# Differential-attention scores as 64-row products on both halves of the array, and the gates' columns turned one pair later

## The chip, the cores and the metric

The kernel runs on one core of a Trainium2 chip. The core has a matrix engine (TensorE; PE in the profile, its weight loads PEld), VectorE (DVE), ScalarE (ACT), GpSimd (POOL) and SyncE (SP), which here issues nearly all DMAs. The metric is the device time of one execution in microseconds, as the median of several runs.

## The reference

One layer on a sequence of 1024 rows and 1024 features: a normalisation, a projection to all segments, two branches (an mLSTM in both directions with 4 heads of 256, and a differential attention with 8 heads), a gated mix of the two, an output projection and a final normalisation. The change is in the attention branch. A head has two query and two key parts (j = 0, 1) of 64 features each, turned by a rotary embedding, and values of 128 features:

```
scores = jnp.einsum('bqhjd,bkhjd->bhjqk', qb, k) * scale
p = jax.nn.softmax(scores, axis=-1)
p_diff = p[:, :, 0] - lam * p[:, :, 1]
return jnp.einsum('bhqk,bkhd->bqhd', p_diff, v)
```

All is in 32-bit floating point.

## The kernel before, in words

**Precision.** A 32-bit product is made of products of a reduced 32-bit type. An operand x is split into a high part H (a rounded copy, by ScalarE) and a low part L = x - H (by GpSimd or VectorE), and a product is taken as HH + HL + LH, three products on TensorE that accumulate in one PSUM bank.

**Stages.** The normalised input stays in SBUF as hH and hL, transposed. First come the mLSTM's projections (`pair_units`, L286), sixteen pairs of weight columns by a scheme with fewer products; pairs alternate between convolution pairs (aq, ak) and output-gate pairs. Small steps are put between these units by a table of (pair, place): the mLSTM's gates (`ml_gates`: rows, chain, weights, columns) and the rotary tables (`ang`). `columns` turns four gate rows blocks and a decay row into columns with 64-row transposes (L131) into banks T and copies them out on VectorE (L810, L817). Then comes the attention (461 to about 1110 us), then the mLSTM, then the two mixes and the output.

**Attention.** `da_proj` makes q and k of a head in two halves of 512 columns (L424 products), turns them (L847 to L865) and leaves them in tile `hl`: partitions 0 to 63 are q of j = 0 and 1, 64 to 127 are k, with 32 rows for each half of the rotation; four slices hold H and L of the two halves. Through a DRAM tile `stk` (four writes, L868) these rows are stacked anew: `qq` gets q's 64 rows of a j twice, on partitions 0 to 63 and again on 64 to 127 (two loads, L870), and `kst` gets H of k on the upper 64 partitions and L of k on the lower ones (L871). So one product of 128 rows with H of q gives HH + HL, and a second with L of q gives LH + LL: four products of 512 columns for the 1024 keys of one j (L918).

For a query tile t of 128 rows, `scores(t, j)` takes a two-bank PSUM tile S (two such tiles exist), makes these four products, takes the negated row maximum (VectorE, L920), the exponential with its row sum (ScalarE, L922), and with j = 1 the combination of both (L927 to L929). `transposes(t, g)` turns half of the combined tile through the single bank T (L131), ScalarE rounds it to pH (L942) and VectorE makes pL (L943). `pv` multiplies with the values for two tiles at a time (L954), `squares`, `finish`, `spread` and `scale` normalise the head's result; `spread` is a DMA that broadcasts a row to all partitions as `rb`, on SP's queue, and `scale` (L997) waits for it.

**Order.** TensorE's order is fixed by a planner, `Weaver`. Each `Unit` has a nominal cost (MM = 0.214 for a product of 512 columns, TP = 0.109 for a transpose), may hold a bank (`tag`, `hold`) and may have to wait a nominal time after another unit (`after`, from the table `LAG`). `da_cycle` lists the units of one tile; `weave` merges that list with the fill (projections of the next head, gates) by which unit is ready first, then by the share of its list that is done. A unit's own costs and holds say nothing to the chip: they set the order alone. The other engines' orders are made by the compiler's scheduler.

Of the kernel before, what the change touches and what calls it, by code (L numbers as in the profile page):

```python
# [28 lines left out]
def two_pi_parts():  # L29
# [9 lines left out]
MM = 0.214  # L39
TP = 0.109  # L40

LAG = dict(Th=2.2, Sh=3.2, PVh=3.7, Mh=8.1, Fh=5.0, qk=14.0, T=6.8, PV=3.7, M=4.5, F=0.4, TTh=1.9, TT=3.2, POh=1.6,
           PO=1.7, Wh=0.3, W=2.0, STh=2.1, ST=4.9, th=1.8, t=4.1, aq=9.0, outh=6.6, out=14.0, G=18.9)


# [64 lines left out]
class Block:  # L110
# [726 lines left out]
    def da_proj(self, h, st):  # L837
        A, v, a, p, q = self.A, self.v, self.a, self.p, self.q
        w1 = self.w1
        fb = lambda x: x.bitcast(F32)  # L840
        kA, kB = ("rope", h, 0), ("rope", h, 1)

        def first(half, pa):
            c = slice(half * 512, (half + 1) * 512)
            m = [w1.tile([128, 512], F32, name=f"m{i}", tag=f"m{i}", bufs=1) for i in range(2)]
            st["m"] = m
            v.tensor_tensor(out=m[0], in0=pa, in1=self.cosT[:, c], op=ALU.mult)  # L847
            v.tensor_tensor(out=m[1], in0=pa, in1=self.sinT[:, c], op=ALU.mult)

        def second(half, pb):  # L850
            c = slice(half * 512, (half + 1) * 512)
            if half == 0:
                st["k"] = w1.tile([128, 2, S], F32R, name="kst", tag="kst", bufs=2)
            qq = w1.tile([128, 4, 512], F32R, name="qq", tag="qq", bufs=3)
            st["q", half] = (qq[:, 0::2], qq[:, 1::2])
            m = st["m"]

            hl = w1.tile([128, 4, 512], F32R, name="hl", tag="hl", bufs=1)
            v.tensor_tensor(out=fb(hl[:, 2]), in0=pb, in1=self.sinT[:, c], op=ALU.mult)
            v.tensor_tensor(out=fb(hl[:, 3]), in0=pb, in1=self.cosT[:, c], op=ALU.mult)  # L860
# [42 lines left out]
    def da_parts(self, h, st):  # L903
        v, a, p, q, w1 = self.v, self.a, self.p, self.q, self.w1

        def scores(t, j):
            if t == 0 and j == 0:
# [3 lines left out]
            qH, qL = st["q", t // 4]  # L911
            c = slice((t % 4) * 128, (t % 4) * 128 + 128)
            Z = st["Z"]
            ps = self.bank("S", (128, S))
            for x, first in ((qH, True), (qL, False)):
                for kh in range(2):
                    o = slice(kh * 512, (kh + 1) * 512)
                    self.t.matmul(ps[:, o], lhsT=x[:, j, c], rhs=st["k"][:, j, o], start=first, stop=not first)  # L918
            nm = w1.tile([128, 1], F32, name="nm", tag="nm", bufs=3)
            v.tensor_reduce(out=nm, in_=ps, axis=AX.X, op=ALU.max, negate=True)  # L920
            e = w1.tile([128, S], F32, name=f"e{j}", tag=f"e{j}", bufs=2 if j == 0 else 1)
            a.activation(out=e, in_=ps, func=AF.Exp, bias=nm[:, 0:1], accum_out=Z[:, j, t:t + 1])  # L922
            st["e", j] = e
            if j == 1:
                e0 = st["e", 0]
                r = w1.tile([128, 1], F32, name="r", tag="r", bufs=1)
                v.reciprocal(out=r, in_=Z[:, 1, t:t + 1])  # L927
                v.tensor_scalar(out=r, in0=r, scalar1=Z[:, 0, t:t + 1], scalar2=self.nlam[:, 0:1], op0=ALU.mult, op1=ALU.mult)
                v.scalar_tensor_tensor(out=e0, in0=e, scalar=r[:, 0:1], in1=e0, op0=ALU.mult, op1=ALU.add)  # L929
                st["p", t] = e0  # L930

        def transposes(t, g):
            pt = st["p", t]
# [61 lines left out]
        def scale(half):  # L995
# [7 lines left out]
        return dict(  # L1003
            S=lambda t, j: Unit(4 * MM, lambda: scores(t, j), tag="S", hold=LAG["Sh"], name=("S", h, t, j), after=((("qk", h), LAG["qk"]),)),
            T=lambda t, g: Unit(4 * TP, lambda: transposes(t, g), tag="T", hold=LAG["Th"], name=("T", h, t, g),
                                after=((("S", h, t, 1), LAG["T"]),)),
            PV=lambda t2, g: Unit(12 * TP, lambda: pv(t2, g), tag="PV" if g == 0 else None, hold=LAG["PVh"], name=("PV", h, t2, g),
                                  after=((("T", h, 2 * t2 + 1, g), LAG["PV"]),)),
            M=lambda t2: Unit(2 * TP, lambda: squares(t2), tag="PV", hold=LAG["Mh"], name=("M", h, t2),
                              after=((("PV", h, t2, 1), LAG["M"]), (("z", h if t2 == 3 else -1), 0.0))),  # L1010
# [3 lines left out]
    @staticmethod  # L1014
    def da_cycle(cur, prev, t):

        before = cur if t > 0 else prev
        un = []
        if cur:
            un.append(cur["S"](t, 0))  # L1020
        own = cur if t >= 4 else prev
        if own and t % 2 == 0:
            un.append(own["M"]((t // 2 - 2) % 4))
        if prev and t in (4, 6):
            un.append(prev["G"](t // 2 - 2))
# [12 lines left out]
        return un  # L1038
# [403 lines left out]
    def build(self):  # L1442
# [21 lines left out]
        with pool(name="const", bufs=1) as self.const, \  # L1464
# [51 lines left out]
            w = Weaver()  # L1516
# [137 lines left out]
```

## Time and profile before

| | us |
|---|---|
| median of 3 runs | 1732.61 (1730.03 to 1735.3) |
| the profiled execution | 1731.73 |
| its span in the profile | 1730.0 |
| mean granted TensorE clock | 0.990 |
| TensorE products busy | 1661.3 (96%) |
| weight loads busy | 1417.5 (82%) |
| VectorE, ScalarE, GpSimd busy | 998.4, 783.6, 603.4 |

A row of instructions in order of time reads: start, shown length, engine, line, operation, out<-in, rows*columns of the weights, and the shape that streams. A product's end is modelled, so consecutive products overlap in the shown lengths; the distance between starts is what a product takes. In a table by stretch the columns are busy time and count of PE, PEld, DVE, ACT and POOL, the granted clock, the DMA share and GB/s.

### The profile page before, as it was taken

To read this page: it belongs to the slowest core of one execution; us is meant where nothing else is said; L and a number is where in the kernel's file an instruction comes from. 1 tells how busy PE (TensorE), PEld (TensorE's weight loads), DVE (VectorE), ACT (ScalarE), POOL (GpSimd) and SP (SyncE) were. 2 spreads that over 40 slices of the span, in tenths; PEclk is the share of its full clock that TensorE was granted. 3 is DMA by queue.
4 is the path that set the end of the run, shared out by engine and by line. 5 is a ranking of instruction groups with operands and counts; after the bars stand their busy time and mean duration, and the time that the engine had idled before them with its cause. 6 is when DMAs were issued, how large, how long until landed. Compare 5 with 4: busy or idle time off the path is not lost. (4 is left out here: it accounts for less than half of the span.)

```text
span 1730.0 us, 24692 instructions
## 1 busy us (share of the span) xinstructions
PE 1661.3 (96%) x9119; PEld 1417.5 (82%) x9119; DVE 998.4 (58%) x1855; ACT 783.6 (45%) x1562; POOL 603.4 (35%) x608
## 2 busy tenths in 40 slices
PE   7999998999999999999999999989999989999998
PEld 5777886887887987898889878879999877888887
DVE  5678677674267666666676665425666743226533
ACT  7455554553245444445545445424655743122221
POOL 4767665665232224322441331222312311222000
PEclk9999999999999999999999999999999999999999
DMA  5343433435443514441635152146455327444222
GB/s 181 93 136 112 143 114 122 122 122 153 126 98 84 144 56 117 117 121 38 170 74 135 44 158 68 61 150 199 140 157 157 89 87 247 143 144 136 86 85 86
DMA packets 190092, 208.15 MB, mean 120 GB/s; under 512 B 12249, under 2 KB 135538, under 8 KB 189970
## 3 DMA queue, kind: packets, MB, share of 16 engines
q1 hardware_dynamic: 189058, 204.98, 40.2%
q8 instruction: 72, 1.18, 0.3%
q10 hardware_dynamic: 912, 1.59, 0.2%
q14 instruction: 50, 0.41, 0.1%
HBM read 143.47 MB, written 63.05 MB: 119 GB/s over the span
## 5 line engine op out<-in xcount | busy, mean ns | idle before, releaser
L424 PE MATMUL pj<-hH,wH 128*128 128x512 f32 x640 | 257.7, 403 | 6.3 <-ACT wH L188 3.1
L424 PE MATMUL pj<-hH,wL 128*128 128x512 f32 x640 | 252.6, 395 | 2.6 <-POOL wL L202 1.7
L424 PE MATMUL pj<-hL,wH 128*128 128x512 f32 x640 | 252.4, 394 | 0.2 <-DVE hL L575 0.2
L922 ACT ACTIVATE e<-S,nm 128x1024 f32<-128x1024 f32 x128 | 143.1, 1118 | 170.2 <-DVE nm L920 169.8
L204 POOL TENSOR_TENSOR wL<-raw,wH 128x1024 fp32r<-128x1024 f32 x41 | 101.0, 2463 | 295.1 <-ACT wH L199 290.2
L920 DVE TENSOR_REDUCE nm<-S 128x1 f32<-128x1024 f32 x128 | 155.7, 1217 | 21.3 <-PE S L918 21.2
L943 DVE TENSOR_TENSOR pL<-T,pH 128x512 fp32r<-128x512 f32 x128 | 87.9, 687 | 138.4 <-ACT pH L942 138.4
L918 PE MATMUL S<-kst,qq 128*128 128x512 f32 x512 | 151.4, 418 | 1.3 <-DMA kst<-stk 1.3
L446 PE MATMUL pj<-wH,hH 128*128 128x256 f32 x512 | 147.7, 288 | 0.3
L424 PEld LDWEIGHTS pj<-hH,wH 128*128 128x128 f32 x640 | 121.6, 190 | 31.1 <-ACT wH L188 3.5
L424 PEld LDWEIGHTS pj<-hH,wL 128*128 128x128 f32 x640 | 121.2, 189 | 30.8 <-POOL wL L202 3.1
L446 PE MATMUL pj<-wL,hH 128*128 128x256 f32 x512 | 145.0, 283 | 1.4 <-POOL wL L202 1.4
L446 PE MATMUL pj<-wH,hL 128*128 128x256 f32 x512 | 144.6, 282 | 0.0
L424 PEld LDWEIGHTS pj<-hL,wH 128*128 128x128 f32 x640 | 121.3, 189 | 23.4 <-DVE hL L575 0.6
L424 PE MATMUL pj<-sl_yb,wH 128*128 128x512 f32 x384 | 120.7, 394 | 4.4 <-ACT sl_yb L1327 2.3
L199 ACT CAST wH<-raw 128x1024 fp32r<-128x1024 f32 x56 | 58.8, 1050 | 120.8 <-PE pj L424 111.1
L918 PEld LDWEIGHTS S<-kst,qq 128*128 128x128 f32 x512 | 90.6, 193 | 15.3 <-DMA kst<-stk 1.8
L446 PEld LDWEIGHTS pj<-wL,hH 128*128 128x128 f32 x512 | 97.7, 191 | 2.3 <-POOL wL L202 2.3
L446 PEld LDWEIGHTS pj<-wH,hH 128*128 128x128 f32 x512 | 97.9, 191 | 1.6 <-ACT wH L199 0.7
L446 PEld LDWEIGHTS pj<-wH,hL 128*128 128x128 f32 x512 | 97.8, 191 | 0.9
L929 DVE SCALAR_TENSOR_TENSOR e<-e,r,e 128x1024 f32<-128x1024 f32 x64 | 94.7, 1480 | 1.3
L189 POOL TENSOR_TENSOR wL<-raw,wH 128x512 fp32r<-128x512 f32 x32 | 40.7, 1290 | 154.5 <-ACT wH L188 149.1
(357 smaller groups left out, 4127.9 us busy)
## 6 DMA issues: line engine op xcount, KB each, us to landing
raw<-in_w_in_dram SPq DMA_DIRECT2D x88, 512.0 KB
stk<-hl SPq DMA_DIRECT2D x64, 256.0 KB
qq<-stk SPq DMA_DIRECT2D x32, 512.0 KB
kst<-stk SPq DMA_DIRECT2D x16, 512.0 KB
x<-in_x_dram SPq DMA_DIRECT2D x8, 512.0 KB
cak<-y SPq DMA_DIRECT2D x16, 256.0 KB
cakH<-cin SPq DMA_DIRECT2D x16, 256.0 KB
cakL<-tz SPq DMA_DIRECT2D x16, 256.0 KB
```

The lines of the kernel that those rows point to most:

```text
L189: self.p.tensor_tensor(out=vw(wL), in0=src, in1=vw(wHf), op=ALU.subtract)
L199: self.a.copy(wH, raw)
L204: self.p.tensor_tensor(out=wL, in0=raw, in1=wHf, op=ALU.subtract)
L424: self.t.matmul(ps, lhsT=l[:, k, :], rhs=r, start=(n == 0), stop=(n == 23))
L446: self.t.matmul(ps[:, i, :], lhsT=l, rhs=r[:, k, :], start=(kh == 0 and k == 0 and m == 0), stop=(kh == 1 and k == 3 and m == 2))
L918: self.t.matmul(ps[:, o], lhsT=x[:, j, c], rhs=st["k"][:, j, o], start=first, stop=not first)
L920: v.tensor_reduce(out=nm, in_=ps, axis=AX.X, op=ALU.max, negate=True)
L922: a.activation(out=e, in_=ps, func=AF.Exp, bias=nm[:, 0:1], accum_out=Z[:, j, t:t + 1])
L929: v.scalar_tensor_tensor(out=e0, in0=e, scalar=r[:, 0:1], in1=e0, op0=ALU.mult, op1=ALU.add)
L943: v.tensor_tensor(out=pL[:, :, s], in0=ps, in1=pH[:, :, s].bitcast(F32), op=ALU.subtract)
```

## The change

`hl` goes to DRAM by (H or L, half of the rotation), one write for each of its four slices over all 128 partitions. `qq` now has H and L of q with j = 0 on the upper 64 partitions and j = 1 on the lower ones, and `kst` has the same for k: one load each. `scores(t)` takes both PSUM tiles and makes for each half of the keys and each of HH, HL and LH one product of 64 rows for j = 0 and one for j = 1, in turns; the product LL is no longer made. Maxima, exponentials and the combination follow as before, both maxima now after one unit. In the planner a tile has one score unit of 6 MM in place of two of 4 MM, S is one holding of 5.0 instead of two of 3.2, and the transposes wait 6.8 after that unit. In `da_cycle` the second score unit between the two transpose units is gone. Apart from this, the five steps of `columns` go from pair 9, places 8 to 12, to pair 10, places 5, 7, 9, 11 and 13, between steps of `ang` at 4 to 12.

```
-            qq = w1.tile([128, 4, 512], F32R, name="qq", tag="qq", bufs=3)
-            st["q", half] = (qq[:, 0::2], qq[:, 1::2])
+            qq = st["q", half] = w1.tile([128, 2, 512], F32R, name="qq", tag="qq", bufs=3)
...
-            dr = self.dram.tile([4, 4, 32, 512], F32, name="stk", tag="stk", bufs=2)
-            for g in range(4):
-                q.dma_start(out=dr[g].rearrange("c i s -> i c s"), in_=fb(hl[32 * g:32 * g + 32]))
-            for o in range(2):
-                q.dma_start(out=fb(qq[64 * o:64 * o + 64]), in_=dr[0:2].rearrange("j (p c) i s -> (c i) (j p) s", p=2))
-            q.dma_start(out=fb(st["k"][:, :, c]), in_=dr[2:4].rearrange("j c i s -> (c i) j s"))
+            dr = self.dram.tile([2, 4, 2, 32, 512], F32, name="stk", tag="stk", bufs=2)
+            for y in range(2):
+                for x in range(2):
+                    q.dma_start(out=dr[y, :, x], in_=fb(hl[:, 2 * y + x]))
+            for i, x in enumerate((qq, st["k"][:, :, c])):
+                q.dma_start(out=fb(x), in_=dr[:, 2 * i:2 * i + 2].rearrange("y j x i s -> (j x i) y s"))
...
-            ps = self.bank("S", (128, S))
-            for x, first in ((qH, True), (qL, False)):
-                for kh in range(2):
-                    o = slice(kh * 512, (kh + 1) * 512)
-                    self.t.matmul(ps[:, o], lhsT=x[:, j, c], rhs=st["k"][:, j, o], start=first, stop=not first)
+            both = [self.bank("S", (128, S)) for _ in range(2)]
+
+            for o in (slice(0, 512), slice(512, S)):
+                for m, (x, y) in enumerate(((0, 0), (0, 1), (1, 0))):
+                    for j, ps in enumerate(both):
+                        r = slice(64 * j, 64 * j + 64)
+                        self.t.matmul(ps[:, o], lhsT=qq[r, x, c], rhs=k[r, y, o], start=(m == 0), stop=(m == 2))
...
-            S=lambda t, j: Unit(4 * MM, lambda: scores(t, j), tag="S", hold=LAG["Sh"], name=("S", h, t, j), after=((("qk", h), LAG["qk"]),)),
+            S=lambda t: Unit(6 * MM, lambda: scores(t), tag="S", hold=LAG["Sh"], name=("S", h, t), after=((("qk", h), LAG["qk"]),)),
...
-            un.append(cur["S"](t, 0))
+            un.append(cur["S"](t))
...
-        if cur:
-            un.append(cur["S"](t, 1))
...
-                                     ((8, 4), 2, weights), ((8, 13), 1, ang[1:2]), ((9, 8), 1, columns), ((10, 4), 2, ang[2:7]),
+                                     ((8, 4), 2, weights), ((8, 13), 1, ang[1:2]), ((10, 4), 2, ang[2:7]), ((10, 5), 2, columns),
...
-            w.banks.update(S=2)
+            w.banks.update(S=1)
```

More of the change, by code (lines that the diff above doesn't have):

```diff
@@ L40 @@
 TP = 0.109
-LAG = dict(Th=2.2, Sh=3.2, PVh=3.7, Mh=8.1, Fh=5.0, qk=14.0, T=6.8, PV=3.7, M=4.5, F=0.4, TTh=1.9, TT=3.2, POh=1.6,
+LAG = dict(Th=2.2, Sh=5.0, PVh=3.7, Mh=8.1, Fh=5.0, qk=14.0, T=6.8, PV=3.7, M=4.5, F=0.4, TTh=1.9, TT=3.2, POh=1.6,
            PO=1.7, Wh=0.3, W=2.0, STh=2.1, ST=4.9, th=1.8, t=4.1, aq=9.0, outh=6.6, out=14.0, G=18.9)
@@ L904, in da_parts, with scores @@
         v, a, p, q, w1 = self.v, self.a, self.p, self.q, self.w1
-        def scores(t, j):
-            if t == 0 and j == 0:
+        def scores(t):
+            if t == 0:
                 st["Z"] = w1.tile([128, 2, 8], F32, name="Z", tag="Z", bufs=2)
@@ L910, in scores @@
                 st["att"] = w1.tile([128, S], F32, name="att", tag="att", bufs=1)
-            qH, qL = st["q", t // 4]
+            qq, k = st["q", t // 4], st["k"]
             c = slice((t % 4) * 128, (t % 4) * 128 + 128)
             Z = st["Z"]
-            ps = self.bank("S", (128, S))
-            for x, first in ((qH, True), (qL, False)):
-                for kh in range(2):
-                    o = slice(kh * 512, (kh + 1) * 512)
-                    self.t.matmul(ps[:, o], lhsT=x[:, j, c], rhs=st["k"][:, j, o], start=first, stop=not first)
@@ L919, in scores @@
[L919 to L930, printed above, removed]
+            both = [self.bank("S", (128, S)) for _ in range(2)]
@@ new lines, in scores @@
+            for o in (slice(0, 512), slice(512, S)):
[3 more added lines that the diff above has]
+                        self.t.matmul(ps[:, o], lhsT=qq[r, x, c], rhs=k[r, y, o], start=(m == 0), stop=(m == 2))
+            for j, ps in enumerate(both):
+                nm = w1.tile([128, 1], F32, name="nm", tag="nm", bufs=3)
+                v.tensor_reduce(out=nm, in_=ps, axis=AX.X, op=ALU.max, negate=True)
+                e = w1.tile([128, S], F32, name=f"e{j}", tag=f"e{j}", bufs=2 if j == 0 else 1)
+                a.activation(out=e, in_=ps, func=AF.Exp, bias=nm[:, 0:1], accum_out=Z[:, j, t:t + 1])
+                st["e", j] = e
@@ L932, in transposes @@
+            e0 = st["e", 0]
+            r = w1.tile([128, 1], F32, name="r", tag="r", bufs=1)
+            v.reciprocal(out=r, in_=Z[:, 1, t:t + 1])
+            v.tensor_scalar(out=r, in0=r, scalar1=Z[:, 0, t:t + 1], scalar2=self.nlam[:, 0:1], op0=ALU.mult, op1=ALU.mult)
+            v.scalar_tensor_tensor(out=e0, in0=e, scalar=r[:, 0:1], in1=e0, op0=ALU.mult, op1=ALU.add)
+            st["p", t] = e0
         def transposes(t, g):
@@ L1003, in da_parts @@
         return dict(
-            S=lambda t, j: Unit(4 * MM, lambda: scores(t, j), tag="S", hold=LAG["Sh"], name=("S", h, t, j), after=((("qk", h), LAG["qk"]),)),
+            S=lambda t: Unit(6 * MM, lambda: scores(t), tag="S", hold=LAG["Sh"], name=("S", h, t), after=((("qk", h), LAG["qk"]),)),
             T=lambda t, g: Unit(4 * TP, lambda: transposes(t, g), tag="T", hold=LAG["Th"], name=("T", h, t, g),
-                                after=((("S", h, t, 1), LAG["T"]),)),
+                                after=((("S", h, t), LAG["T"]),)),
             PV=lambda t2, g: Unit(12 * TP, lambda: pv(t2, g), tag="PV" if g == 0 else None, hold=LAG["PVh"], name=("PV", h, t2, g),
```

## The prediction

> **What bounds the kernel now.** I read the busy times of the engines first, then the busy times by stretch, then who waited for whom, then single instructions in order of time.
>
> ```profile
> span 1730.0 us, 24692 instructions
> PE 1661.3 (96%) x9119; PEld 1417.5 (82%) x9119; DVE 998.4 (58%) x1855; ACT 783.6 (45%) x1562; POOL 603.4 (35%) x608
> 461.00:1101.00 640.00, 622.88 (x3596) 537.99 (x3595) 412.29 (x599) 319.45 (x659) 199.68 (x125) 0.99 0.38 100
> ```
>
> TensorE bounds the program, and also the stage that the change rewrites: from 461 to 1101 us, where the 512 score products run, it shows 622.9 of 640 us, VectorE 412, ScalarE 319 (columns: PE, PEld, DVE, ACT, POOL). That stage pays for TensorE time first and for TensorE's waits second:
>
> ```profile
> PE PV L954 <- DVE pL L943: 6.5, 3, 2.4
> PE T L131 <- DVE gc_negM L810: 4.7, 1, 4.7
> PE T L131 <- DVE pL L943: 4.3, 11, 0.5
> PE pj L424 <- ACT wH L188: 3.1, 1, 3.1
> PE S L918 <- DMA kst<-stk: 1.3, 1, 1.3
> ```
>
> (Columns: total us, times, longest.) The second row belongs to the gates' columns, the other four to the attention stage, 15.2 us together; of these I move only the last two or three by reasoning, the rest is order.
>
> **The score products, before.** A score unit of one j is four products of 128 rows by 512 columns:
>
> ```profile
> 630.94 1.08 PE L918 MATMUL S<-kst,qq 128*128 128x512 f32 x4
> 631.86 0.39 PE L424 MATMUL pj<-hH,wH 128*128 128x512 f32 x1
> 704.23 0.60 PE L131 MATMUL T<-ident,e 128*128 128x128 f32 x4
> 704.59 1.18 PE L918 MATMUL S<-kst,qq 128*128 128x512 f32 x4
> 705.60 0.39 PE L424 MATMUL pj<-hH,wH 128*128 128x512 f32 x1
> L131 PE MATMUL T<-ident,e 128*128 128x128 f32 x512 | 78.7, 277 | 5.4 <-DVE pL L943 4.3 <-DVE zz L970 0.6 <-DVE e L929 0.5
> ```
>
> Shown lengths overlap, so I go by starts. 630.94 to 631.86 is 0.92 us, 0.23 a product. Behind transposes the pair of groups takes 705.60 - 704.23 = 1.37; four transposes at 0.11 (0.60 less a shown length of 0.27, over three steps) leave 0.93. A query tile t has two such units: 1.85 us, and 64 tiles make 118 us.
>
> **After.** Twelve products of 64 rows, alternating between the halves. If the halves stream together there are six rounds of 0.23 = 1.38 us, because a round still streams 512 columns. That alone would give 64 x (1.85 - 1.38) = 30 us. But a change between 128-row and 64-row products has a price, and the kernel has five places where it shows: the gates' columns are transposed as 64-row products between 128-row ones.
>
> ```profile
> 259.59 0.39 PE L286 MATMUL T<-hH,wH 128*128 128x512 f32 x1
> 259.90 0.14 PEld L131 LDWEIGHTS T<-ident,gch 64*128 64x128 f32 x1 [0.35 <-issue]
> 259.96 0.14 PEld L131 LDWEIGHTS T<-ident,gch 64*128 64x128 f32 x1
> 260.02 0.22 PE L131 MATMUL T<-ident,gch 64*128 64x64 f32 x1
> 260.17 0.19 PEld L286 LDWEIGHTS T<-TH,wL 128*128 128x128 f32 x1
> 260.28 0.19 PEld L286 LDWEIGHTS T<-TL,wL 128*128 128x128 f32 x1
> 260.51 0.40 PE L286 MATMUL T<-TL,wL 128*128 128x512 f32 x1
> 260.51 0.19 PEld L286 LDWEIGHTS T<-TH,wL 128*128 128x128 f32 x1
> ```
>
> Usually the load for the next product starts with the running product (260.51 and 260.51). Here the first 64-row load waits 0.31 us after the product at 259.59, nobody's semaphore being named ("issue"). The two 64-row loads are 0.06 apart, the 128-row ones at 260.17 and 260.28 are 0.11 apart, so I take a load as 0.06 and 0.11. Way in: 0.31 + 0.06 = 0.37 to the next product instead of 0.23, cost 0.14. Way out: the load at 260.17 starts 0.15 after the last 64-row transpose, whose 64 columns stream for 0.03; so some 0.1 us of emptying, as on the way in (0.31 - 0.23). After 512 columns that is 0.23 + 0.09 = 0.32, plus an exposed load of 0.11 = 0.43 instead of 0.23, cost 0.20. The second half starts one load, 0.06, behind the first. Sum per tile: 1.38 + 0.14 + 0.20 + 0.06 = 1.78, against 1.85: 0.07 x 64 = **4.5 us gained**, not 30. Behind transposes instead of 512-column products the way in is the same up to 0.02.
>
> The unknown term is the round. No row has two halves at once. Bounds from rows: 0.23 (full overlap) and 0.46 (none: two products of 0.23). I take 0.23, because the 64-row load takes half as long as the 128-row one (0.06 against 0.11), which says that such an instruction occupies half of the array. A round decides where it costs more than (1.85 - 0.40)/6 = 0.24; from there on the products lose.
>
> The Trainium skill ("TensorEngine Tiling (Array Packing)", Key Properties) says that row tiles work independently in load and product, but that changing the tiling mode drains TensorE; the 0.31 us above is such a drain. Its page "TensorE: Matmul & The Clock Gate" (LDWEIGHTS) makes a load's time depend on columns alone, not on rows; that would be rival 5 below, in which the products gain nothing. The 0.06 between the loads at 259.90 and 259.96 speaks against it here.
>
> **The chain behind a score unit.** Both maxima now follow one unit.
>
> ```profile
> L920 DVE TENSOR_REDUCE nm<-S 128x1 f32<-128x1024 f32 x128 | 155.7, 1217 | 21.3 <-PE S L918 21.2
> L922 ACT ACTIVATE e<-S,nm 128x1024 f32<-128x1024 f32 x128 | 143.1, 1118 | 170.2 <-DVE nm L920 169.8
> L929 DVE SCALAR_TENSOR_TENSOR e<-e,r,e 128x1024 f32<-128x1024 f32 x64 | 94.7, 1480 | 1.3
> L943 DVE TENSOR_TENSOR pL<-T,pH 128x512 fp32r<-128x512 f32 x128 | 87.9, 687 | 138.4 <-ACT pH L942 138.4
> L942 ACT CAST pH<-T 128x512 fp32r<-128x512 f32 x125 | 73.1, 585 | 38.7 <-PE T L131 35.6
> ```
>
> The banks come free after two maxima and an exponential, 2 x 1.22 + 1.12 = 3.6 us plus hops; the planner keeps 5.0. The probabilities come 1.48 later, one maximum later than before, and the unchanged 6.8 covers 5.1 plus hops. The stage gives a tile 640/64 = 10 us, in which the projections still fill. The first product of a tile now waits for both exponentials of the tile before; behind it on TensorE stand the fill and the transposes. So both waits are covered; without the fill the next scores would wait those 3.6 us. What loses cover is the T bank: the two transpose units of a tile no longer have a score unit between them, only fill up to a planned 2.2 us. I charge 2 us for that (range 0 to 20, rival 3).
>
> **The stacking DMAs.**
>
> ```profile
> stk<-hl SPq DMA_DIRECT2D x64, 256.0 KB
> qq<-stk SPq DMA_DIRECT2D x32, 512.0 KB
> kst<-stk SPq DMA_DIRECT2D x16, 512.0 KB
> ```
>
> Four writes stay, each now one piece of all 128 partitions; the q loads halve (16 issues and 8 MB less). They lie under 10 us tiles; only the first scores wait for them, 1.3 us in the waits above. I count 1 us gained at most, 0 taken. Queued among them on SP is the broadcast rb, which stalls three heads alike:
>
> ```profile
> 687.28 0.75 DVE L997 SCALAR_TENSOR_TENSOR zg<-zg,cols,rb 128x512 f32<-128x512 f32 x1 [1.65 <-DMA rb<-rsd]
> 690.48 0.39 PE L954 MATMUL PV<-pL,vH 128*128 128x256 f32 x1 [2.39 <-DVE pL L943]
> 692.00:697.00 5.00, 5.00 (x20) 3.95 (x18) 2.08 (x3) 1.63 (x5) 0.00 (x0) 0.66 1.05 275
> ```
>
> VectorE waits for rb in order, the low halves pL behind it are late, and TensorE waits 2.39; after it the granted clock is 0.66 over 5 us, another 1.7. Whether the new order keeps rb behind the stk writes I can't tell: taken as unchanged, rival 4 otherwise.
>
> **The gates' columns.**
>
> ```profile
> 264.83 4.05 DVE L368 SCALAR_TENSOR_TENSOR pj<-cin,cols,pj 128x512 f32<-128x512 f32 x6
> 265.45 0.40 PE L286 MATMUL T<-hH,wH 128*128 128x512 f32 x1
> 270.55 0.44 PE L131 MATMUL T<-ident,gch 64*128 64x64 f32 x2 [4.70 <-DVE gc_negM L810]
> 270.92 0.79 PE L286 MATMUL T<-hH,wH 128*128 128x512 f32 x1
> 275.78 0.40 PE L286 MATMUL T<-TL,wL 128*128 128x512 f32 x1
> 285.00:290.00 5.00, 5.00 (x24) 4.07 (x22) 4.86 (x13) 1.25 (x2) 0.00 (x0) 1.00 0.27 83
> 268.00:276.00 8.00, 5.45 (x14) 3.84 (x15) 4.48 (x14) 3.65 (x6) 5.66 (x5) 0.57 0.65 211
> ```
>
> The copies of the columns stand behind seven convolution steps on VectorE, and the bank is late: 4.7 us. Behind it the granted clock is 0.57 (last row), and 270.92 to 275.78 holds nine products and a transpose, 4.86 us for 9 x 0.23 + 0.46 = 2.5: another 2.3. One pair later the products are of a convolution pair whose own VectorE work comes after, but the angles are there and keep VectorE at 4.86 of 5 us. With two slots of six products, 1.4 us each, between columns the copies have time; I leave 0.5 us. Gain 4.7 + 2.3 - 0.5 = **6.5 us** (bounds 0, if the wait only moves, and 7).
>
> **Sum.** 4.5 + 6.5 - 2 = 9 us off the profiled execution's 1731.73 us (span 1730.0 and 1.7 around it): 1722.7. That execution lies 0.9 under the median of 1732.61, so I say **1723**; its own range, with the round at 0.225 to 0.25 and stalls of 5 either way, is 1713 to 1733.
>
> **Rivals.** (1) *The halves don't overlap*, that is, the change doesn't do what it says: round 0.46, unit 6 x 0.46 + 0.34 = 3.1, loss 1.25 x 64 = 80, less the columns: 1805. For it: no row shows overlap. Against it: the half-length loads. Half-way, at a round of 0.30, 1722.7 + 64 x 6 x 0.07 = 1750. (2) *The switch is free* for these plain products, the drain being a matter of the transposes: unit 1.38 + 0.06, gain 26 + 6.5 - 2: 1701. Against it: the 128-row transposes switch from and to products without it (0.93 above). (3) *The T bank takes the place*: a maximum (1.22) or the combination (1.48) stands before pL, emptying takes 0.59 + 0.69 + 1.3 = 2.6 or more instead of the planned 2.2; a wait of 0.5 in most of the 64 tiles is 25 in place of 2: 1746. It decides from 0.17 us a tile, where it eats the 11 us. For it: pL's 138 us of waiting for pH; against it: 11 such waits, the longest 0.5, so far. (4) *The rb stalls vanish*: 6.5 us of waits (three, in the table of waits) and 3 x 1.7 of clock, 12 us: 1711. (5) *A 64-row load takes 0.11 like the others*: way in and stagger 0.05 longer each, unit 1.88, the products lose 2 us: 1729. Against it: 0.06 between the two loads.
>
> **Chances.** Forecast 0.41; no or half overlap 0.17; free switch 0.15; T bank 0.12; rb 0.10; long loads 0.05. A measurement tells about 0.3%, 5 us, from no change. Forecast (most), free switch and rb are faster: 0.60; the forecast's upper end, the long loads and part of the T bank are the same: 0.19; the rest slower: 0.21. The range 1696 to 1752 holds all but no overlap and a little of the tails.
>
> **What would show it.** Score products 64*128, 768 of them, starts alternating by about 0.06 and 0.17; a load that starts 0.3 us after the last 128-row product before them and a gap of about 0.4 behind them; 1.8 us a tile. The wait on gc_negM gone. Wrong, if pairs of score products are 0.46 apart (rival 1), if the loads don't pause (2), or if T waits for pL over 15 us in all (3).

## The result, and the profile after

The changed kernel takes 1825.88 us (median, 1822.44 to 1828.77) against 1733.28 us (1730.03 to 1735.3) of the kernel before on the same chip: a ratio of 1.0533, 95% interval 1.0517 to 1.0548, some 93 us **slower**. The prediction said 1723, and its range ended at 1752. Times here and below are medians of ordinary executions; left out are one of the run with the order alone (1907.07 us, granted clock 0.839) and one of run (d) (9210.55 us).

The page of the changed kernel begins like this (span, then the busy times of the engines):

```profile
span 1823.1 us, 25192 instructions
PE 1680.3 (92%) x9375; PEld 1398.9 (77%) x9375; DVE 1008.8 (55%) x1855; ACT 781.3 (43%) x1562; POOL 591.3 (32%) x608
```

The span grew by 93.1 us. TensorE's products are busy for 19.0 us more, and the time in which none runs grew from 68.7 to 142.8 us, by 74.1. So TensorE stands still more, and what it does takes longer; the mean granted clock fell from 0.990 to 0.968. The table of TensorE's waits (total us, times, longest) names one wait for nearly all of it:

```profile
PE T L131 <- DVE pL L944: 93.1, 33, 10.6
```

Before, the same row read 4.3 us, 11 times, at most 0.5. The wait on `gc_negM` is gone from the table.

**The products themselves** came out as forecast. The group of the score products, and one unit in order of time:

```profile
L919 PE MATMUL S<-kst,qq 64*128 64x512 f32 x768 | 119.9, 448 | 0.2 <-ACT e L924 0.2
```

```profile
629.90 0.60 PE L131 MATMUL T<-ident,e 128*128 128x128 f32 x4
630.42 1.66 PE L919 MATMUL S<-kst,qq 64*128 64x512 f32 x12
632.02 0.51 PE L424 MATMUL pj<-hH,wH 128*128 128x512 f32 x1
632.36 0.39 PE L424 MATMUL pj<-hL,wH 128*128 128x512 f32 x1
```

The row that follows the prediction's last row of before, for comparison (the one ahead of it starts at 705.60):

```profile
705.83 0.40 PE L424 MATMUL pj<-hL,wH 128*128 128x512 f32 x1
```

To the start of the next product it is 632.02 - 629.90 = 2.12 us, less 0.44 for the four transposes 1.68. But that product is held up as well: its successor starts 0.34 us behind it (632.36), where before it was 0.23 (705.60 to 705.83). With these 0.11 us a tile takes 1.79 us, against 1.85 before. The starts of the twelve products, read one by one from the trace, are:

```
630.425 630.428   630.763 630.766   630.994 630.997
631.230 631.233   631.458 631.461   631.691 631.694   then 632.02 632.36
```

The two halves start 3 ns apart, and a round is 0.23 us: they overlap fully. The rest is the way in, 0.08 us behind the transposes and 0.10 in the first round (0.335 instead of 0.23), and the way out, 0.10 to the next product (0.33 instead of 0.23) and 0.11 behind it. Counted in this way over all units that the traces show at full clock and with no wait beside them, the median is 1.79 us a tile after (50 tiles) and 2 x 0.935 = 1.87 before (120 units). So the products gain 0.06 to 0.08 us a tile, 4 to 5 us over 64 tiles. This is worked out from rows; no run has the products alone.

**The long waits.** Six times, at intervals of about 97 us, the first at 578.2 us, TensorE's second transpose unit of a tile waits about 10 us. This is the first of them, rows in order of time:

```profile
572.21 3.87 SPq L868 DMA_DIRECT2D stk<-hl  x4
574.71 0.66 PE L131 MATMUL T<-ident,e 128*128 128x128 f32 x4 [0.18 <-DVE pL L944]
576.19 2.23 SPq L994 DMA_DIRECT2D rb<-rsd  x1
577.95 0.28 PE L446 MATMUL pj<-wL,hH 128*128 128x256 f32 x1
587.29 0.75 DVE L998 SCALAR_TENSOR_TENSOR zg<-zg,cols,rb 128x512 f32<-128x512 f32 x1 [8.88 <-DMA rb<-rsd]
588.14 0.68 DVE L944 TENSOR_TENSOR pL<-T,pH 128x512 fp32r<-128x512 f32 x1
588.88 1.12 PE L131 MATMUL T<-ident,e 128*128 128x128 f32 x4 [10.64 <-DVE pL L944]
```

SP issues the four writes of `stk` and, directly behind them, the broadcast `rb` of the head before. `rb` lands some 11 us after its issue at 576.19. VectorE, which works in order, stands for 8.88 us at `scale`, which needs `rb`; `pL` of the first transpose is queued behind that, the single T bank stays taken, and the second transpose, at the head of TensorE's queue, waits 10.64 us. What the DMA engines do meanwhile (columns as in the tables by stretch: PE, PEld, DVE, ACT, POOL, granted clock, DMA share, GB/s):

```profile
576.00:578.00 2.00, 2.00 (x19) 2.00 (x17) 0.91 (x1) 2.00 (x3) 0.00 (x0) 1.00 0.26 99
580.00:582.00 2.00, 0.00 (x0) 0.00 (x0) 0.00 (x0) 0.00 (x0) 0.00 (x0) 0.85 0.34 120
582.00:584.00 2.00, 0.00 (x0) 0.00 (x0) 0.00 (x0) 0.00 (x0) 0.00 (x0) 0.50 0.26 102
584.00:586.00 2.00, 0.00 (x0) 0.00 (x0) 0.00 (x0) 0.00 (x0) 0.00 (x0) 0.50 0.24 93
```

From 580 to 586 us no engine computes, and the DMA engines are busy to a quarter for most of it, at about 100 GB/s. In the stretch that the prediction shows of before, at 692 to 697, the DMA engines moved 275 GB/s at a share of 1.05. The granted clock falls to 0.50 during the idle time, so the work behind the wait starts slowly too: the four transposes at 588.88 show 1.12 us, those at 574.71 0.66.

### The profile page after: what moved, and what is told of

It reads as the page before. It is cut to its first block, busy times and chain, and to the rows that moved or that the text cites. A ratio compares the mean times of both kernels' runs of the same rounds, so it can differ in the third digit from the quotient of the medians.

```text
span 1823.1 us, 25192 instructions
## 1 busy us (share of the span) xinstructions
PE 1680.3 (92%) x9375; PEld 1398.9 (77%) x9375; DVE 1008.8 (55%) x1855; ACT 781.3 (43%) x1562; POOL 591.3 (32%) x608
## 5 line engine op out<-in xcount | busy, mean ns | idle before, releaser
L424 PE MATMUL pj<-hH,wH 128*128 128x512 f32 x640 | 270.5, 423 | 3.8 <-DVE hl L859 1.9
L131 PE MATMUL T<-ident,e 128*128 128x128 f32 x512 | 83.0, 287 | 93.3 <-DVE pL L944 93.1
L922 DVE TENSOR_REDUCE nm<-S 128x1 f32<-128x1024 f32 x128 | 150.5, 1218 | 20.1 <-PE S L919 19.0
L131 PEld LDWEIGHTS T<-ident,e 128*128 128x128 f32 x512 | 62.1, 146 | 115.3 <-DVE pL L944 107.7
L943 ACT CAST pH<-T 128x512 fp32r<-128x512 f32 x128 | 74.9, 585 | 108.3 <-PE T L131 107.1
L919 PE MATMUL S<-kst,qq 64*128 64x512 f32 x768 | 119.9, 448 | 0.2 <-ACT e L924 0.2
```

Of the source, the lines that this page charges most:

```text
L131: self.t.transpose(out, in_, self.ident[0:k, 0:k])
L424: self.t.matmul(ps, lhsT=l[:, k, :], rhs=r, start=(n == 0), stop=(n == 23))
L919: self.t.matmul(ps[:, o], lhsT=qq[r, x, c], rhs=k[r, y, o], start=(m == 0), stop=(m == 2))
L943: a.copy(pH[:, :, s], ps)
```

## The experiments

Each time stands against the kernel before on the same chip. "After" is the changed kernel.

**The writes.** First: after, with the `stk` writes as before (32 partitions each), and loads to match (four of 256 KB in place of two of 512).

```
-            dr = self.dram.tile([2, 4, 2, 32, 512], F32, ...)
-                    q.dma_start(out=dr[y, :, x], in_=fb(hl[:, 2 * y + x]))
+            dr = self.dram.tile([4, 4, 32, 512], F32, ...)
+                q.dma_start(out=dr[g].rearrange("c i s -> i c s"), in_=fb(hl[32 * g:32 * g + 32]))
...
+                for j in range(2):
+                    q.dma_start(out=fb(x[64 * j:64 * j + 64]), in_=dr[2 * i + j].rearrange("(y x) i s -> (x i) y s", y=2))
```

> The changed kernel, but the rotated q and k go to DRAM as before the change: four writes of 32 partitions with four slices each, into a DRAM tile laid out by 32-row group; the two loads become four of 64 partitions and 256 KB. The score products and the order stay those of the change. Theory W (the new writes, whose outermost dimension is 4, run on a quarter of the DMA engines: share 0.24 to 0.26 and about 100 GB/s while they run; the broadcast rb stands behind them, VectorE waits for rb, pL stands behind that on VectorE, and the second transpose unit of the tile waits for the T bank): the share while stk is written rises to 0.5 or more, the wait of T for pL falls from 93 us to under 30, time 1715 to 1745. Theory O (the order alone: the two transpose units stand next to each other on one bank, whatever rb does): the wait of T for pL stays over 60 us, time 1790 or more.

Measured: 1762.5 us, ratio 1.0156 (1.0135 to 1.0178). Its waits, and its DMA share in two stretches in which such writes run:

```profile
PE T L131 <- DVE pL L944: 42.9, 33, 3.2
```

```profile
572.00:574.00 2.00, 1.76 (x15) 1.55 (x13) 0.63 (x3) 2.00 (x7) 0.00 (x0) 1.00 0.92 193
574.00:576.00 2.00, 0.00 (x0) 0.00 (x0) 1.97 (x3) 1.03 (x5) 0.00 (x0) 1.00 0.96 248
```

The share is 0.92 to 0.96, no wait for `pL` is longer than 3.2 us, and 63 us are back. 43 us of these waits are left. The result lies between the two theories: the writes were the larger part, but time and waits stayed above theory W's ranges.

Then the reverse: before, with the form of the writes alone.

```
-                q.dma_start(out=dr[g].rearrange("c i s -> i c s"), in_=fb(hl[32 * g:32 * g + 32]))
+                q.dma_start(out=dr[:, g], in_=fb(hl[:, g]))
```

> The kernel before with the write form of the change alone: four writes, one for each slice of hl over 128 partitions, outermost dimension 4; the DRAM tile, the loads, the products and the order stay. Theory W: the DMA share falls to about 0.25 while they run, rb lands later. With a score unit between the transposes the waits are paid at PV and at the transposes as far as rb comes late: 1745 to 1790. If the writes hurt only through the order of the change: 1731 to 1740.

Measured: 1839.94 us, ratio 1.0609 (1.0585 to 1.0634). One line of the old kernel costs 105 us, far above the expected range. Its waits:

```profile
PE T L131 <- DVE pL L943: 45.9, 14, 12.9
PE S L918 <- DMA kst<-stk: 23.2, 3, 7.9
PE PV L954 <- ACT pH L942: 22.5, 3, 7.6
PE pj L446 <- DVE zg L878: 9.3, 2, 8.7
```

These four make 100.9 us. In the old order the same lateness shows in more places, the first scores of a head among them.

How do the writes reach TensorE? After, with the slow writes, but `scale` multiplies with a table that is always there, so that VectorE never waits for `rb`:

```
-            v.scalar_tensor_tensor(out=g, in0=g, scalar=self.subln, in1=st["rb"], op0=ALU.mult, op1=ALU.mult)
+            v.scalar_tensor_tensor(out=g, in0=g, scalar=self.subln, in1=self.cosT[:, half * 512:(half + 1) * 512], op0=ALU.mult, op1=ALU.mult)
```

> The changed kernel, with one wait taken away: the scaling of a head's result multiplies with a slice of the cosine table instead of the broadcast rb (so the normalisation of the attention's heads is left out of the result; the broadcast is still made). Slow writes and order stay. If VectorE's wait for rb is the only way in which the writes cost time: the waits of 10 us disappear, T for pL under 30 us, time 1715 to 1740. If the late qq and kst cost time of their own, or the transposes' order does: 1750 or more.

Measured: 1766.38 us, ratio 1.0181 (1.0159 to 1.0203).

```profile
PE T L131 <- DVE pL L944: 47.5, 34, 4.9
```

That is the first experiment's time within 4 us, though the writes are slow. In the changed kernel the writes therefore cost by way of `rb` and VectorE's order, and hardly otherwise. What keeps this run above 1750 is also there with the fast writes, so it isn't the writes.

**The columns.** Before, with the columns moved alone (the line of the table of small steps in the diff above).

> The kernel before with one part of the change alone: the gates' columns one pair later. By the prediction's step: the wait of T for gc_negM (4.7 us) and the half clock behind it go, 6.5 us less: 1725 to 1729. If the wait only moves: 1731 to 1735.

Measured: 1726.87 us, ratio 0.9952 (0.9934 to 0.9969): 8.9 us gained, 5.4 to 11.5 by the interval. This beats both kernels, and none of the other complete versions reached it. Its page shows TensorE busy for 7.4 us less than before, and about as much idle time:

```profile
span 1722.2 us, 24689 instructions
PE 1653.9 (96%) x9119; PEld 1410.9 (82%) x9119; DVE 1002.5 (58%) x1855; ACT 782.0 (45%) x1562; POOL 601.6 (35%) x608
```

Between these two profiled executions most of the gain is the clock, granted at 0.995 on the mean here against 0.990: 1661.3 x 0.990 / 0.995 = 1653. The split is less sure than the gain, since the granted clock of the kernel before itself lies between 0.987 and 0.993 from execution to execution. The 4.7 us of wait on `gc_negM` are gone, but the first scores of a head now wait 4.0 us more for `kst`:

```profile
PE S L918 <- DMA kst<-stk: 5.3, 3, 2.7
```

**The order.** Does the transposes' place cost the rest? Before, with the order of the change alone: one unit of eight 128-row products with a holding of 5.0, then both maxima and exponentials; writes, loads and columns of before.

```
-            S=lambda t, j: Unit(4 * MM, lambda: scores(t, j), tag="S", hold=LAG["Sh"], name=("S", h, t, j), ...),
+            S=lambda t: Unit(8 * MM, lambda: scores(t), tag="S", hold=LAG["Sh"], name=("S", h, t), ...),
...
-            un.append(cur["S"](t, 0))
+            un.append(cur["S"](t))
-        if cur:
-            un.append(cur["S"](t, 1))
```

> The kernel before with the order of the change alone: one score unit for both j (the eight products of 128 rows, then both maxima, exponentials and the combination), its hold and waits in the planner as in the change, no score unit between the transposes; products, DMAs and columns stay those of before. Theory O2 (what is left of the loss in the kernel with the spread writes, 1762, is the order: the low halves pL of the first transpose unit stand behind two maxima, two exponentials and the combination, and the second transpose unit waits for the one T bank): T for pL 35 to 60 us, time 1765 to 1785. Rival (it is the 64-row products that bring it, by their own time): T for pL as before, 4 us, time 1730 to 1740.

Measured: 1805.84 us, ratio 1.0428 (1.0388 to 1.0469), more than was expected.

```profile
PE T L131 <- DVE pL L951: 70.2, 37, 6.2
```

Here nothing is changed but the order, and the T bank takes 70 us. What such a wait looks like, in the first experiment's kernel (old writes, new order), the longest one; rows of three engines in order of time:

```profile
632.03 1.11 ACT L924 ACTIVATE e<-S,nm 128x1024 f32<-128x1024 f32 x1
632.21 0.60 PE L131 MATMUL T<-ident,e 128*128 128x128 f32 x4
633.40 1.11 ACT L924 ACTIVATE e<-S,nm 128x1024 f32<-128x1024 f32 x1
634.49 0.59 ACT L943 CAST pH<-T 128x512 fp32r<-128x512 f32 x1
635.48 0.17 DVE L143 TENSOR_TENSOR rb_w<-rb_y 128x8 f32<-128x8 f32 x1 [1.77 <-POOL rb_y L142]
636.87 1.28 DVE L930 SCALAR_TENSOR_TENSOR e<-e,r,e 128x1024 f32<-128x1024 f32 x1
638.07 0.68 DVE L944 TENSOR_TENSOR pL<-T,pH 128x512 fp32r<-128x512 f32 x1
638.81 1.11 PE L131 MATMUL T<-ident,e 128*128 128x128 f32 x4 [3.22 <-DVE pL L944]
```

The first transposes start at 632.21, beside the first exponential. `pH` stands behind both exponentials on ScalarE and starts at 634.49. It is done at 635.08, but `pL` starts only at 638.07: on VectorE a short chain for the head's normalisation, which waits 1.77 us for GpSimd, and the combination stand ahead of it. TensorE has run out of fill by then.

Attempts to give the T bank its cover back. (a) After, the first transposes ahead of the score unit, so that the products lie between the two transposes again:

```
         if cur: ...
+        if before:
+            un.append(before["T"]((t - 1) % 8, 0))
             un.append(cur["S"](t))
-        if before:
-            un.append(before["T"]((t - 1) % 8, 0))
```

> The changed kernel, but the first transpose unit of the tile before stands ahead of the score unit, the second behind it (a score unit between them again); writes stay slow. If the T bank's single buffer turns VectorE's wait for rb into TensorE's wait: pL of the first unit is then ahead of the scaling on VectorE, T for pL falls under 30 us, and TensorE waits for late pL at PV instead, some 2 to 5 us each at six or more places as in the kernel before: 1735 to 1770. If the order is irrelevant and the 10 us wait reaches TensorE on any way: over 1790.

Measured: 1828.26 us, ratio 1.0532 (1.0508 to 1.0556): nothing gained.

```profile
PE T L131 <- DVE e L930: 51.3, 12, 14.3
PE T L131 <- DVE pL L944: 42.5, 24, 8.8
```

The first transposes now come before their probabilities are there. (b) The first experiment, with the planner keeping the T bank for 5.0 instead of 2.2 (`Th`):

> The changed kernel with the spread writes of the earlier run, and the planner told that a transpose unit holds its bank for 5.0 in place of 2.2, so that more fill stands between the two units. Theory O2: T for pL falls from 43 us to under 15, time 1725 to 1740. If the fill only moves the wait to the scores or to PV: 1750 or more.

Measured: 1787.42 us, ratio 1.0309 (1.0283 to 1.0334). T waits for `pL` 59.7 us, all at second transposes. Counted from the trace, 35 of the 64 tiles now have about 5.5 us of products between the two and wait 0.3 us in all, while 25 tiles have 0.7 us or none there and wait 55.6: where the plan kept the room the theory held, but it left others without any. (c) The first experiment, with the second maximum, exponential and the combination as a unit of their own behind the first transposes:

```
+            weigh(t, 0)
+        def weigh(t, j):
...
+            S1=lambda t: Unit(0.0, lambda: weigh(t, 1)),
...
+            un.append(cur["S1"](t))
```

> The changed kernel with the spread writes, and the second maximum, exponential and the combination emitted behind the first transpose unit of the tile (the products of both j stay together in front). VectorE then has pL of the first unit between the two maxima, as before the change. Theory O2: T for pL under 12 us, time 1715 to 1730, faster than both kernels. Rival (the scores' banks are then held longer and the next scores wait): S for the exponential over 15 us, 1740 or more.

Measured: 1748.72 us, ratio 1.0083 (1.0057 to 1.011): 14 us better than the first experiment, with the same order on TensorE, yet above the 1730 at which the theory's range ended.

```profile
PE T L131 <- DVE pL L950: 36.2, 34, 2.9
```

(d) The same with `Th` at 3.4:

> The changed kernel with the spread writes and the second maximum, exponential and combination behind the first transpose unit, as in the last run of that kind (1748.7, T for pL 36 us in 34 waits, most of 1.0 to 1.4), and the planner's hold of a transpose unit at 3.4 in place of 2.2. Theory (the planned distance between the two transpose units is too short, since a score unit of 0.86 no longer stands there): most of the waits near 1 us go, T for pL under 20 us, time 1725 to 1740. Rival (the fill is moved from elsewhere, and the wait only goes to the other side of the pair, as with the hold of 5.0): T for pL 30 us or more, 1745 or more.

Measured: 1752.96 us, ratio 1.0104 (1.0076 to 1.0132), in the rival's range; no profile shows its waits. (e) The first experiment with (a) and the transposes due 8.5 instead of 6.8 after the scores:

> The changed kernel with the spread writes, the first transpose unit of the tile before ahead of the score unit and the second at the end of the tile, and the transposes planned 8.5 in place of 6.8 after the scores. Theory (pL of the first unit is then ahead of the two maxima on VectorE, and the other transpose unit comes a tile's work later): T for pL under 15 us, T for the combined tile e under 15 us, time 1715 to 1735. Rival (the scores come so late in the tile that e isn't ready for the next first unit): T for e over 25 us, 1745 or more.

Measured: 1823.4 us, ratio 1.0508 (1.0478 to 1.0538). T waits for the combined tile 51.9 us and for `pL` 35.2 us. (f) The first experiment with (a) and the second exponential's unit behind `pv`:

> As the run before with the first transpose unit ahead of the score unit, and also the second maximum, exponential and combination emitted behind the products with the values, with the transposes planned 6.8 after the scores and 5.5 after that step. Theory: both bursts on VectorE are broken up, T for pL under 10 us, time 1712 to 1730, the gain of the 64-row products (0.16 us a tile, 10 us) and of the columns (9 us) together. Rival (the scores' banks are held by the second exponential until late, and the next scores wait): S for the exponential over 10 us, 1735 or more.

Measured: 1779.66 us, ratio 1.0261 (1.0234 to 1.0289). None of (a) to (f) did what its theory said. In (a) and (e) most of the wait moved to the first transposes of a tile, in (f) it stands at both, in (b) it stayed at the second.

(g) The order of before, kept as it was: all twelve products in the first score slot, and a unit of 4 MM in the plan, with the second maximum, exponential and combination but no product, where the second score unit stood. Old writes, new columns.

```
+            S=lambda t: Unit(4 * MM, lambda: scores(t), tag="S", hold=LAG["Sh"], name=("S", h, t, 0), ...),
+            S1=lambda t: Unit(4 * MM, lambda: weigh(t, 1), tag="S", hold=LAG["Sh"], name=("S", h, t, 1), ...),
```

> All twelve products of a head pair's unit run in the first score slot on both halves, the rows are written and loaded as before, the columns are turned one pair later; the maxima, exponentials and combination of the second tile of scores stand as a unit of their own where the second score unit stood, and every due time of before is kept. Theory (the order behind the products cost the rest, and with the order of before the products' 0.16 us a tile, 10 us, and the columns' 9 us are both seen): TensorE's T waits for pL under 15 us in all, 1712 to 1725, below the kernel before and below the columns alone. Rival (TensorE no longer has the second products between its two transposes, so the second transpose comes too soon for pL of the first, or the next products wait for the second exponential): T for pL or S for e over 20 us, 1730 to 1745.

Measured: 1748.03 us, ratio 1.0087 (1.0069 to 1.0105): the rival, 3 us above its range.

```profile
PE T L131 <- DVE pL L950: 34.9, 21, 3.2
PE S L919 <- ACT e L928: 2.4, 2, 1.8
```

The expectation counted 10 us for the products; by the rows above they gain 4 to 5. With the columns' 9 that is some 13 us, and the wait for `pL` grows by 31, with every due time of before: 18 us of loss, where 15 were measured. The plan still counts the second unit at 4 MM, but no product stands there: counted from the trace, TensorE has 2.1 us of products between the two transposes in 47 of the 64 tiles, where it had 3.0 before, and these tiles have 29.9 of the 34.9 us.

**Which engine makes pL late?** Each suspect was shortened by itself. VectorE, by a combination over 128 of 1024 columns, in the first experiment's kernel and in (g):

```
-            v.scalar_tensor_tensor(out=e0, in0=e, scalar=r[:, 0:1], in1=e0, ...)
+            v.scalar_tensor_tensor(out=e0[:, 0:128], in0=e[:, 0:128], scalar=r[:, 0:1], in1=e0[:, 0:128], ...)
```

> As with the products on both halves and the spread writes (1762.5 us, T for pL 42.9 us), but the combination takes 128 of the 1024 columns of the second exponentials (the other 896 columns of a tile's weights stay the first softmax alone): VectorE loses about 1.1 us a tile, ScalarE and TensorE lose nothing. Theory V (pL is late behind the combination on VectorE): T for pL falls below 20 us and the time to 1730 to 1742. Theory A (pH is late behind the exponentials on ScalarE): T for pL stays at 35 to 43 us, 1755 to 1764.

> All products in the first score slot, the due times of before kept (1748.0 us, T for pL 34.9 us), and the combination over 128 of the 1024 columns (the rest of the weights stays the first softmax alone). Theory V: T for pL below 15 us, 1718 to 1730, since the products' 10 us and the columns' 9 us are then seen. Rival: T for pL stays at 30 us or more, 1740 to 1748.

ScalarE, by a second exponential over 128 columns:

```
-                a.activation(out=e, in_=ps, func=AF.Exp, ...)
+                    a.activation(out=e[:, 0:128], in_=ps[:, 0:128], func=AF.Exp, ...)
```

> As with the products on both halves and the spread writes (1762.5 us, T for pL 42.9 us), but the second exponential of a tile is taken over 128 of its 1024 columns, and the combination, of the same size as before, uses the first exponentials twice: ScalarE loses about 0.9 us a tile, and the combination comes that much sooner. Theory A: T for pL falls below 20 us, 1730 to 1742. Theory V: the combination stays ahead of pL, only 0.9 us sooner; T for pL 25 to 35 us, 1745 to 1757.

Measured: 1741.38 us (ratio 1.0041, 1.0025 to 1.0057) with the short combination, 1747.0 us (1.0073, 1.005 to 1.0096) with the short exponential, 1726.04 us (0.9957, 0.9941 to 0.9973) with the short combination in the order of before. Their rows, one fence each, in this order:

```profile
PE T L131 <- DVE pL L944: 32.9, 31, 2.3
```

```profile
PE T L131 <- DVE pL L947: 34.4, 34, 2.3
```

```profile
PE T L131 <- DVE pL L950: 17.2, 19, 1.8
```

In the new order either one takes 8 to 10 us from the wait of 42.9 and 15 to 21 us from the time. In the order of before the combination makes half of the wait: 17.7 of 34.9 us, and 22 us of time. All three times fell into theory V's ranges (1741.38 at the edge), but with the short combination the waits stayed above what V said, 32.9 and 17.2 where it wanted less than 20 and 15. The short exponential doesn't single out ScalarE, since it also brings the combination sooner. What tells the two apart is how long `pL` stands after its `pH` is done, with other work of VectorE ahead of it. Summed from the trace over the waits, that accounts for up to 22 of the first experiment's 43 us; in the other 21 `pH` itself is late. So both queues make `pL` late, and neither alone. In (g) it is 22 and 13 us, and with the short combination 6 and 11. Even there the kernel is no faster than the columns alone: its 17 us of waits for `pL` are 13 more than theirs, against the products' 4 to 5 us and some 11 us of other waits that it lost (PV for `pL` 6.0, the scores for `kst` 5.3).

## Why the prediction was wrong, by its own steps

**The score products: right, in part by luck.** Six rounds of 0.23, as said. The forecast's terms of 0.14 for the way in, 0.20 for the way out and 0.06 for the stagger measured 0.18, 0.21 and 0.003. So a tile takes 1.79 us where 1.78 was forecast, and the gain is 4 to 5 us where 4.5 was. Two terms were off and cancel: the stagger fell away (no row says why), and the way in is longer, because in the first round the second load of a half starts 0.11 us behind the first (630.423 and 630.531), not the 0.06 that the forecast took. The range of 1713 to 1733 doesn't follow from its own terms: a round of 0.225 to 0.25 is 1.9 us less to 7.7 more, which with 5 us of stalls either way gives 1716 to 1735. Rival 1 (no overlap) and rival 2 (free switch) are out; of rival 5 the 0.11 for a load fits this row, but its unit of 1.88 is out. The Trainium skill ("TensorE: Matmul & The Clock Gate", Part 3 on packing small matmuls) lets products on different row groups start about 4 ns apart; the 3 ns here agree.

**The gates' columns: the size right, the reason in part.** 8.9 us measured alone, with an interval that holds the forecast of 6.5. The split differs: I put more than half on the wait, and took the stretch from 270.92 to 275.78 for nine products where the trace has ten, which makes the clock's term 2.1 and not 2.3. The wait went, but idle time hardly fell (68.7 to 68.3 us), as the scores' wait for `kst` grew, and busy time fell by 7.4.

**"Four writes stay, each now one piece of all 128 partitions … 1 us gained at most, 0 taken": this step failed.** I looked at the count and size of the transfers, not at their shape. The step cost 63 us in the changed kernel (undone, with the loads that go with it) and 105 in the old one (the writes alone). A write to `dr[y, :, x]` has the four groups of 32 rows (q and k, two j each) as its slowest dimension, of size 4, where the old one had the 32 partitions. The trace shows a DMA share of a quarter against 0.92 to 0.96. The Trainium skill ("DMA: Bandwidth & Descriptors", "Why a DMA increments its semaphore by 16 and not by 1") says that a transfer is spread over the largest number of engines, up to 16, that divides the slowest dimensions of both sides: 4 here, and 4 of 16 is the quarter that the rows show. The rule was there to be read, and it spoke against the change. That it is this dimension, and nothing else in the writes' shape, rests on the share and the rule: no run changed the dimension by itself.

**"Whether the new order keeps rb behind the stk writes I can't tell: taken as unchanged": this failed with it.** I saw the queue, SP's writes ahead of `rb`, and VectorE's wait in order, and gave only the gain (rival 4) a price. Its loss has the same place: `rb` now takes 11 us, and the 10.64 us above are that. With `rb`'s wait taken away, the kernel with the slow writes is 4 us from the one with the fast ones.

**"I charge 2 us for that (range 0 to 20, rival 3)": too small, and its range too.** Rival 3 was the right mechanism, at 25 us of wait, and the prediction's own sign for it (over 15 us) came. In the new order with the old writes it is 42.9 us, and with order alone changed 70.2. The prediction looked for the loss in the cover, but the fill kept most of that: in most tiles of the first experiment 2.8 us of products stand between the two transposes, 3.0 before. What it mis-sized is the emptying. It was counted as pH, pL and one VectorE instruction; in the longest wait the rows show it behind two exponentials, the combination, and a chain that waits for GpSimd, 6.6 us from one transpose to the next. From the start of the first transposes to the end of `pL` the median over the tiles is 2.7 us in the first experiment, above 4 in a fifth of them, against 2.0 before. And more than the wait can be lost: between the profiled executions of the first experiment and of its shortened combination, 10.0 us less wait were 19.0 us less time, with the clock granted at 0.986 and 0.991 on the mean. In the pair made from (g), 17.7 were 18.4.

**The parts don't add up singly**: writes alone cost 105 us, order alone 72, both with some 13 us of gains 93. In the changed kernel both are paid at the same place, `pL` before the second transpose. That the order's 1 to 3 us lie inside VectorE's 9 us at `rb` there is argued from the rows at 587.29, not tried by itself.

**Still open.** Why the order alone costs more with 128-row products (1805.84) than with 64-row ones on both halves (1762.5, of which products and columns explain some 13 of 43 us). And how the last 17 us of waits for `pL` divide: ScalarE's queue and the lack of a score unit between the transposes are both left, and no run took both away. A second T bank was not tried; no run shows what it would be worth.

## What to carry to other kernels

When a stacking DMA is rewritten, compare the slowest dimension of both its sides before and after, not the count or the bytes: a neat write with a 4 outermost ran at a quarter of the DMA share and cost more than the whole change could gain. Then look who stands behind it in its queue and which in-order engine waits for that one; a broadcast that nobody thinks of was the way from a DMA to TensorE. And when two units of work are merged into one, what they hand to the other engines comes in one burst as well: a single-bank hand-over needs the whole queue of each evacuating engine in its sum, not the evacuations alone. Last, when a switch of shape is priced from rows, count on until the distances are normal again: half of the way out stood behind the first product after the unit.

## What the hardware showed that I had not expected

- Two 64-row products on the two halves start 3 ns apart, and the price of going from 128-row to 64-row products and back is 0.39 us a visit (0.18 in, 0.21 out), half of the way out paid by the second product behind it. The transposes of the gates' columns had suggested 0.34.
- Four DMAs of 256 KB whose slowest dimension was 4, and the broadcast behind them, held the DMA share at 0.24 to 0.34, at 93 to 120 GB/s, while all engines stood still; the same bytes written with 32 as the slowest dimension ran in stretches at 0.92 to 0.96, at 193 to 248 GB/s.
- The clock's share in a wait: around the 10.64 us the mean granted clock over 2-us stretches was 0.85 and then 0.50, and a microsecond less of wait for `pL` went with 1.9 us less time in one pair of profiled executions and 1.0 in another.
